# RWKV preparation of a two-block model: 24 parts on half-unit slots, and work moved between GpSimd, VectorE and ScalarE

## The chip, the cores and the metric

The kernel runs on one core of a Trainium2 chip. The metric is the device time of one execution in microseconds (us), the median of several runs. The core's engines run side by side, each with a queue of its own that it works off in order: PE (TensorE), DVE (VectorE), ACT (ScalarE), POOL (GpSimd) and SP, which here only starts DMAs.

## The reference

A model in fp32 with two blocks: block 1 (a pooling mixer and HGRN2) and block 2 (memory attention, a conformer convolution, a bidirectional RWKV-7 scan, an output projection, and a mixture of 16 experts chosen by the experts). The change lies in the RWKV scan of block 2, which for 6 heads of 64 and 1024 tokens computes, in both directions:

```python
def wkv7_scan(r, w, k, v, kk, a, reverse):
    def step(state, inp):
        r_t, w_t, k_t, v_t, kk_t, a_t = inp
        sa = jnp.einsum('bhij,bhj->bhi', state, -kk_t)
        state = (state * w_t[..., None, :]
                 + sa[..., :, None] * (kk_t * a_t)[..., None, :]
                 + v_t[..., :, None] * k_t[..., None, :])
        y_t = jnp.einsum('bhij,bhj->bhi', state, r_t)
        return state, y_t
...
    for d, (wd, ad) in enumerate(((wdf, adf), (wdb, adb))):
...
        k_d = heads(k * (1.0 + (a - 1.0) * k_a.astype(f32)))
        ys = wkv7_scan(r_tm, tm(heads(w)), tm(k_d), v_tm, kk_tm, tm(heads(a)), reverse=(d == 1))
        outs.append(jnp.moveaxis(ys, 0, 1))
        bonuses.append(jnp.sum(r_h * k_d * r_k32, axis=-1, keepdims=True) * v_h)
```

## The kernel before

The two directions run together, one on each half of the 128 partitions. The 1024 tokens are cut into 16 blocks of 64, which are the 16 **steps** of a chain: within a block the recurrence is solved with matrices, and only the state S (64x64 for each head) goes from one step to the next. Two steps make a **unit** g (0 to 7).

**`rwkv_prep`** (line 925) makes a unit's matrices ahead of its steps. It is a generator in 22 parts. Part 0 loads r, k, kk, a (L938) and the decay logs C (L940). Part 1 clears two blocks of AR on POOL (L943), sums C by a scan on DVE (L944), takes exponentials on ACT (L947, L948), forms kd on ACT (L950, six instructions) and multiplies it by k on POOL (L951). Parts 2 to 5 are products of 64 or 128 partitions by 768: AR (L955, L965, L966) and BK (L960, L969) on DVE; a times E (L956) and zz (L962, L963) on POOL. Parts 6 to 9 are the score matmuls on PE (L976), their copies Dt on ACT (L983) and the masked results on DVE (L984, L987). Part 10 writes Dt to DRAM (dD, L999, two DMAs), part 11 reads it back as the 96 triangular 16x16 blocks L (L1007), so that part 12 can invert them all at once: X is cleared on POOL (L1021, L1022), and 15 rounds of a product el (L1028) and a subtraction (L1030) follow. That elimination runs on the engine `el`: DVE for units 0 to 2, POOL for units 3 to 7 (`s.elp`). The inverses go out to DRAM (dX, L1033) and come back spread over 128 partitions (Xc, L1037, two DMAs). The rest builds the inverse M of each 64x64 block from them: Xs on ACT (L1040), a transpose (L1042), matmuls (L1051, L1057), a predicated copy (L1059), a transpose (L1061), four copies into M on DVE (L1063), two more matmuls (L1069, L1076) and the last copies into M on ACT (L1079).

**`rwkv_chain`** (line 1081) does the two steps of a unit: u = AR times A on PE (L1107), its copy us on ACT (L1110), sa = M times us (L1114), its copy B, one half on DVE (L1116) and one on ACT (L1117), then the new state's increment (L1121) and the output y (L1127), S on DVE (L1134, L1135), and the next step's A from S, half on DVE (L1136), half on ACT (L1137). So each step needs M of its unit at L1114, between us and B.

**The order.** `rwkv` (line 1146) walks over slots n, six to a unit, two yields of the chain in each; `s.lead[k]` says how many slots before the unit's first slot part k runs, and `s.fill` in which slots pieces of another stage, the output projection of attention and convolution (`mix_out_a`: loads, L869 and L149 to L151), come. The framework then reorders instructions within a window by its own priorities, so what stands in each engine's queue is shown below. Three register sets (`nset`) let units overlap. A unit's DMAs before the change all start on SP, in one queue with the loads of the next units, the loads of A and B (L1093) and the output writes.

After the last step the output normalisation of the last blocks, routing and the experts follow; they need all of the scan's output.

## Time and profile before

| | |
|---|---|
| median of 3 runs | 3227.86 us (3224.34 to 3228.44) |
| the profiled execution's own time | 3216.67 us |
| its span | 3214.9 us |
| busy over the span | PE 2997.3 (93%), DVE 2269.2 (71%), ACT 1254.0 (39%), POOL 264.8 (8%) |
| mean granted TensorE clock | 0.96 |
| first scan of unit 0 (L944) | 2121.8 us |
| state updates (L1134) | 15, the first at 2216.0, the last at 2480.7 us |

The profiled execution took 11.2 us less than the median. PE is at full speed nearly all the time outside the RWKV stretch; in it, from 2121.8 to about 2504 us, no engine is. A step lasts from 9 to 30 us, and the state update on DVE marks it.

### The profile page before, as it was taken

The numbers are of one execution on the slowest core, as the hardware profiler recorded it, in microseconds if no ns is written. First come the engines' busy times: TensorE is split into PE (matmuls) and PEld (weight loads), VectorE is DVE, ScalarE is ACT, GpSimd is POOL, SyncE is SP. The second block draws the span as 40 slices with busy tenths as digits, with TensorE's granted clock in tenths as the row PEclk, the third lists the DMA queues.
The fourth block names the chain that finished last, engine by engine and source line by source line (L and its number), as shares of the span: only waits on it lengthen the run. The fifth ranks groups of instructions, "written<-read, shape, count | busy, mean of one in ns | idle before, by whom it ended". The sixth has DMA issues, their size and how long they took to land.

```text
span 3214.9 us, 48713 instructions
## 1 busy us (share of the span) xinstructions
PE 2997.3 (93%) x20104; PEld 2457.3 (76%) x20104; DVE 2269.2 (71%) x2774; ACT 1254.0 (39%) x1598; POOL 264.8 (8%) x357
## 2 busy tenths in 40 slices
PE   8999999989999999999998899958878759999998
PEld 6888888778888888888887776646666548888776
DVE  5454545557686766867667897567676689999998
ACT  4221212233222222222223325533344348888777
POOL 0000000000000000000001100032362000000100
PEclk9999999999999999999999999979878779999999
DMA  4111111111111111111111524366744759999994
GB/s 131 46 53 46 47 46 59 40 34 34 40 34 53 41 34 40 34 51 36 40 40 53 130 69 148 115 194 195 196 117 129 280 219 383 383 389 390 379 364 161
DMA packets 349103, 423.88 MB, mean 132 GB/s; under 512 B 84816, under 2 KB 271824, under 8 KB 348880
## 3 DMA queue, kind: packets, MB, share of 16 engines
q1 hardware_dynamic: 342784, 399.26, 37.0%
q0 software_dynamic: 6096, 21.50, 2.5%
q8 instruction: 158, 2.59, 0.3%
q14 instruction: 65, 0.53, 0.1%
HBM read 359.96 MB, written 60.74 MB: 131 GB/s over the span
## 4 chain that ended last, share of the span: by engine, by line
PE 75%; DVE 10%; DMA 5%; ACT 3%; issue 3%; POOL 2%; SPq 1%; DVEq 0%; ACTq 0%; POOLq 0%
PE mm L159 14%; PE mm L161 14%; PE mm L157 14%; PE sc L157 4%; PE sc L161 4%; PE sc L159 4%; PE mm L149 3%; PE mm L151 3%; PE mm L150 3%; DVE cv L681 2%; DVE wl L102 2%; PE sc L404 1%; PE sc L481 1%; PE sc L471 1%; DMA wr<-in_w_e_down_dram 1%
## 5 line engine op out<-in xcount | busy, mean ns | idle before, releaser
L102 DVE TENSOR_TENSOR wl<-wr,wh 128x1024 fp32r<-128x1024 f32 x508 | 608.7, 1222 | 375.9 <-ACT wh L101 356.1
L101 ACT ACTIVATE wh<-wr 128x1024 fp32r<-128x1024 f32 x508 | 530.6, 1059 | 775.4 <-PE mm L159 549.7
L157 PE MATMUL mm<-hn,wh 128*128 128x512 f32 x1600 | 514.8, 395 | 3.3 <-ACT hn L195 1.7
L161 PE MATMUL mm<-hn,wl 128*128 128x512 f32 x1600 | 517.1, 395 | 0.0
L159 PE MATMUL mm<-hn,wh 128*128 128x512 f32 x1600 | 511.0, 394 | 0.0
L161 PEld LDWEIGHTS mm<-hn,wl 128*128 128x128 f32 x1600 | 300.3, 188 | 66.0 <-issue 5.3
L159 PEld LDWEIGHTS mm<-hn,wh 128*128 128x128 f32 x1600 | 300.1, 188 | 66.0 <-issue 4.8
L157 PEld LDWEIGHTS mm<-hn,wh 128*128 128x128 f32 x1600 | 299.7, 189 | 65.9 <-ACT hn L195 2.1
L240 DVE TENSOR_TENSOR h<-sc,h 128x1024 f32<-128x1024 f32 x192 | 229.8, 1219 | 90.2 <-PE sc L161 88.0
L159 PE MATMUL mm<-wl,th 128*128 128x512 f32 x768 | 245.8, 401 | 6.0 <-DVE wl L102 5.9
L157 PE MATMUL mm<-wh,th 128*128 128x512 f32 x768 | 240.3, 394 | 2.3 <-ACT th L101 2.3
L161 PE MATMUL mm<-wh,tl 128*128 128x512 f32 x768 | 238.3, 391 | 0.1
L159 PEld LDWEIGHTS mm<-wl,th 128*128 128x128 f32 x768 | 138.3, 188 | 47.1 <-DVE wl L102 20.8
L161 PEld LDWEIGHTS mm<-wh,tl 128*128 128x128 f32 x768 | 144.3, 188 | 32.2 <-DVE tl L102 0.5
L157 PEld LDWEIGHTS mm<-wh,th 128*128 128x128 f32 x768 | 142.8, 189 | 32.4 <-ACT th L101 2.9
L157 PE MATMUL sc<-oh,sh 128*128 128x512 f32 x512 | 163.2, 395 | 2.2 <-DVE h L240 2.2
L161 PE MATMUL sc<-oh,sl 128*128 128x512 f32 x512 | 159.1, 394 | 0.0
L159 PE MATMUL sc<-ol,sh 128*128 128x512 f32 x512 | 158.6, 391 | 0.0
L149 PE MATMUL mm<-wh,hn 128*128 128x256 f32 x512 | 147.0, 287 | 0.2 <-DVE gt L514 0.2
L151 PE MATMUL mm<-wh,hn 128*128 128x256 f32 x512 | 146.0, 285 | 0.0
L150 PE MATMUL mm<-wl,hn 128*128 128x256 f32 x512 | 145.4, 284 | 0.1
L101 ACT ACTIVATE oh<-wr 128x1024 fp32r<-128x1024 f32 x32 | 33.9, 1059 | 211.9 <-PE sc L161 199.5
(514 smaller groups left out, 4874.2 us busy)
## 6 DMA issues: line engine op xcount, KB each, us to landing
wr<-in_w_e_gate_dram SPq DMA_DIRECT2D x128, 512.0 KB, 7.8
wr<-in_w_e_up_dram SPq DMA_DIRECT2D x128, 512.0 KB, 6.6
wr<-in_w_e_down_dram SPq DMA_DIRECT2D x128, 512.0 KB, 6.4
wr<-in_hgrn_w_in_dram SPq DMA_DIRECT2D x64, 512.0 KB, 4.0
wr<-in_pool_w_in_dram SPq DMA_DIRECT2D x32, 512.0 KB, 4.0
wr<-in_w_in_dram SPq DMA_DIRECT2D x20, 512.0 KB, 3.8
wr<-in_pool_w_out_dram SPq DMA_DIRECT2D x16, 512.0 KB, 3.6
wr<-in_hgrn_w_out_dram SPq DMA_DIRECT2D x16, 512.0 KB, 3.6
```

Source lines behind the costliest of these rows:

```text
L101: s.act(hi, raw, AF.Copy)
L102: (eng or s.V).tensor_tensor(lo, raw, hi.bitcast(F32), op=OP.subtract)
L149: s.mm(o, ah, bh, start=first, stop=False)
L150: s.mm(o, ah, bl, start=False, stop=False)
L151: s.mm(o, al, bh, start=False, stop=last)
L157: s.mm(o, ah, bh[n], start=first, stop=False)
L159: s.mm(o, ah, bl[n], start=False, stop=False)
L161: s.mm(o, al, bh[n], start=False, stop=last)
L240: s.tt(h[i], o, h[i], op=OP.add)
L404: mm(o[r, c], lh[:, c * 128 + n * 64:c * 128 + n * 64 + 64], r3[:, 2 * c + n], start=True, stop=True)
L471: mm(pu[:, cs(c)], kt[:, cs(c)], v[:, c], start=True, stop=True)
L681: s.stt(acc, up[:, t:t + T], w, acc, op0=OP.mult, op1=OP.add)
```

## The change

It does five things.

1. The slots are halved: `lead` counts half slots (a part can now run at either yield of the chain), and the inverse is cut in three by two more yields (after rounds j = 4 and 9), which makes 24 parts. In half slots the numbers before were 30, 24, 24, 24, 24, 22, 22, 20, 16, 14, 14, 14, 6, 6, 6 and seven times 2. `fill` is doubled, which leaves its places.
2. The products kd, a times E and zz go from POOL to DVE (zz behind the masks).
3. `s.elp` is empty: the elimination of every unit runs on DVE.
4. The four copies into M and DVE's half of B go to ACT.
5. The inverse's DMAs (dD, L, dX, Xc, six for each unit) start from POOL's queue rather than SP's.

POOL keeps the memsets. Line numbers move by one up to the scan and by three or so behind it.

```diff
@@ -41,14 +41,15 @@
         s.cnat, s.dmc, s.dmv, s.dmt = 5, s.P.dma_start, s.dma, s.P.dma_start
         s.ahead, s.npf = [], 1
         s.ready = {3: 33, 4: 30, 2: 37, 5: 37, 1: 43, 6: 42}
-        s.elp = (3, 4, 5, 6, 7)
+        s.elp = ()
         s.wo_at, s.wo_done = 38, False
         s.ylast, s.fast, s.dmy = {}, 42, s.dma
         s.nraw, s.nraw2 = 17, 11
         s.n = 0
+        s.dmi = s.P.dma_start
         s.spr, s.nset = 6, 3
-        s.lead = (15, 12, 12, 12, 12, 11, 11, 10, 8, 7, 7, 7, 3, 3, 3, 1, 1, 1, 1, 1, 1, 1)
-        s.fill = (-10, -10, -8, -8, -7, -4, -3, -2, 1, 2, 2, 2, 3, 4, 4, 7, 8, 8, 9, 9, 10)
+        s.lead = (30, 24, 24, 23, 22, 22, 21, 20, 19, 18, 17, 15, 13, 12, 11, 10, 8, 6, 5, 4, 3, 2, 1, 1)
+        s.fill = (-20, -20, -16, -16, -14, -8, -6, -4, 2, 4, 4, 4, 6, 8, 8, 14, 16, 16, 18, 18, 20)
         s.ct = (5, 5, 8)
         s.nye, s.nhid, s.nwh = 1, 2, 3
         s.nsum = 4
@@ -948,19 +949,16 @@
         act(E, C[:, :, 1:], AF.Exp, scale=0.606531)
         for h in range(6):
             act(kd[:, h], a[:, h], AF.Identity, scale=s.rka[:, h:h + 1], bias=s.rkam[:, h:h + 1])
-        s.P.tensor_tensor(kd, x["k"], kd, op=OP.mult)
+        tt(kd, x["k"], kd, op=OP.mult)
         yield
         s.V.tensor_copy(sc.rearrange("p c h -> p h c"), P.rearrange("p (h c) t -> p h c t", c=2)[:, :, :, 64])
         for d, r in enumerate(s.halves):
             tt(AR[r, :, d, 0], u3(x["kk"])[r], P[r, :, 0:64], op=OP.mult)
-        s.P.tensor_tensor(u3(a), u3(a), E, op=OP.mult)
+        tt(u3(a), u3(a), E, op=OP.mult)
         yield
         BK = s.tl(p, "BK", 2, (128, 12, 2, 64))
         for d, r in enumerate(s.halves):
             tt(BK[r, :, 1 - d], u3(kd)[r], E[r], op=OP.mult)
-        zz = s.tl(p, "zz", 1, (128, 6, 128))
-        s.P.tensor_tensor(zz[0:64], x["r"][0:64], kd[0:64], op=OP.mult)
-        s.P.tensor_tensor(rev(zz[64:128]), x["r"][64:128], kd[64:128], op=OP.mult)
         yield
         tt(AR[0:64, :, 0, 1], u3(x["r"])[0:64], P[0:64, :, 1:], op=OP.mult)
         tt(rev(AR[64:128, :, 1, 1]), u3(x["r"])[64:128], P[64:128, :, 1:], op=OP.mult)
@@ -993,10 +991,13 @@
             nx = scores(q + 1) if q < 2 else None
             masked(q, o)
             o = nx
+        zz = s.tl(p, "zz", 1, (128, 6, 128))
+        tt(zz[0:64], x["r"][0:64], kd[0:64], op=OP.mult)
+        tt(rev(zz[64:128]), x["r"][64:128], kd[64:128], op=OP.mult)
         yield
         dD = s.tl(s.dp, "dD", 2, (2, 12 * 4160))
         for d, r in enumerate(s.halves):
-            s.dma(bass.AP(tensor=dD.tensor, offset=dD.offset + d * 12 * 4160, ap=[[64, 64], [4160, 12], [1, 64]]), Dt[r])
+            s.dmi(bass.AP(tensor=dD.tensor, offset=dD.offset + d * 12 * 4160, ap=[[64, 64], [4160, 12], [1, 64]]), Dt[r])
         os = []
         for q in range(2):
             os.append(g_((128, 4, 128)))
@@ -1004,7 +1005,7 @@
                 s.PE.transpose(os[q][:, c], BK[:, 4 * q + c].rearrange("p n t -> p (n t)"), s.ident)
         yield
         L = s.tl(p, "L", 1, (96, 16, 16))
-        s.dma(L, bass.AP(tensor=dD.tensor, offset=dD.offset, ap=[[1040, 96], [64, 16], [1, 16]]))
+        s.dmi(L, bass.AP(tensor=dD.tensor, offset=dD.offset, ap=[[1040, 96], [64, 16], [1, 16]]))
         for q in range(2):
             act(TK[:, 4 * q:4 * q + 4], os[q], AF.Copy)
         o, o1 = g_((128, 4, 128)), g_((128, 6, 2))
@@ -1028,13 +1029,15 @@
             el.tensor_tensor(zv, L[:, j:j + 1, j + 1:].to_broadcast([96, n, m]),
                              X[:, 0:n, j:j + 1].to_broadcast([96, n, m]), op=OP.mult)
             el.tensor_tensor(X[:, 0:n, j + 1:], X[:, 0:n, j + 1:], zv, op=OP.subtract)
+            if j in (4, 9):
+                yield
         yield
         dX = s.tl(s.dp, "dX", 2, (96, 256))
-        s.dma(dX, X.rearrange("p a b -> p (a b)"))
+        s.dmi(dX, X.rearrange("p a b -> p (a b)"))
         yield
         Xc, Xs = s.tl(p, "Xc", 1, (128, 12, 16)), s.tl(p, "Xs", 1, (128, 12, 32))
         for d, r in enumerate(s.halves):
-            s.dma(Xc[r], bass.AP(tensor=dX.tensor, offset=dX.offset + d * 48 * 256, ap=[[16, 64], [1024, 12], [1, 16]]))
+            s.dmi(Xc[r], bass.AP(tensor=dX.tensor, offset=dX.offset + d * 48 * 256, ap=[[16, 64], [1024, 12], [1, 16]]))
         yield
         for n in range(2):
             act(Xs[:, :, n * 16:n * 16 + 16], Xc, AF.Copy, scale=s.m16[:, n:n + 1])
@@ -1060,7 +1063,7 @@
         Xt = s.tl(p, "Xt", 1, (128, 12, 32))
         s.V.transpose(f2(Xt), f2(Xf))
         for n, r in enumerate(quads):
-            s.V.tensor_copy(M[r, :, n % 2 * 32:n % 2 * 32 + 32], Xf[r])
+            act(M[r, :, n % 2 * 32:n % 2 * 32 + 32], Xf[r], AF.Copy)
         yield
         ys = s.tl(p, "ys", 1, (128, 12, 32))
         o = i_()
@@ -1113,7 +1116,7 @@
             for h, d, r in heads:
                 mm(sa[r, h], M[r, 2 * h + c], uv[r, h], start=True, stop=True)
             yield
-            s.V.tensor_copy(B[0:64, 0], sa[0:64])
+            act(B[0:64, 0], sa[0:64], AF.Copy)
             act(B[64:128, 1], sa[64:128], AF.Copy)
             yield
             so = s.tl(ps, "c", 1, (128, 6, 64))
@@ -1146,11 +1149,11 @@
     def rwkv(s, ps, psc, rb, ry):
 
 
-        lead = s.lead
+
         at = {}
         for g in range(8):
-            for k, l in enumerate(lead):
-                at.setdefault(s.spr * g - l, []).append((k, g))
+            for k, l in enumerate(s.lead):
+                at.setdefault(2 * s.spr * g - l, []).append((k, g))
         preps = [s.rwkv_prep(g, ps) for g in range(8)]
         with s.pool("RF", "right") as pf:
             out = s.mix_out_a(psc, pf)
@@ -1164,12 +1167,13 @@
             for n in range(min([*at, *s.fill]), 0):
                 parts(n)
             chain = (x for g in range(8) for x in s.rwkv_chain(g, psc))
-            last = max(s.fill) + 1
+            last = max(s.fill) // 2 + 1
             n = 0
             while n < last:
                 next(chain)
-                parts(n)
+                parts(2 * n)
                 next(chain)
+                parts(2 * n + 1)
                 n += 1
             for _ in out:
                 pass
@@ -1181,7 +1185,7 @@
                 live.remove(b)
 
         for _ in chain:
-            parts(n)
+            parts(2 * n)
             if n == s.wo_at:
                 live.insert(0, s.mix_weights())
             live += [s.mix_block(i, ps, psc) for i, at_ in s.ready.items() if at_ == n]
@@ -1196,6 +1200,7 @@
                 s.prefetch(s.npf)
             step()
             next(chain)
+            parts(2 * n + 1)
             if n >= s.fast:
                 step()
             n += 1
```

In each excerpt a name is a buffer (its number tells instances apart), and the bracket is what the instruction waits for.

**POOL**, before: the end of unit 4's elimination, then the memsets and products of the next unit, and the elimination of unit 5.

```order
L1028 TENSOR_TENSOR el_17512<-L_17301,X_17470 96x28 [waits Pool_49]
L1030 TENSOR_TENSOR X_17470<-X_17470,el_17512 96x14x2 [waits Pool_49]
L1028 TENSOR_TENSOR el_17515<-L_17301,X_17470 96x15 [waits Pool_49]
L1030 TENSOR_TENSOR X_17470<-X_17470,el_17515 96x15 [waits Pool_49]
L1021 MEMSET X_18471 96x256 [waits DMAHW5_49,Pool_49]
L1022 MEMSET X_18471 96x16 [waits Pool_49]
L943 MEMSET AR_1662_14919 64x12x64 [waits PE_49,Pool_49]
L943 MEMSET AR_1662_14919 64x12x64 [waits PE_49]
L951 TENSOR_TENSOR kd_17833<-xk_17526,kd_17833 128x768 [waits DVE_49,DMAHW2_49,Activation_49,Pool_49]
L956 TENSOR_TENSOR xa_17530<-xa_17530,EX_17832 128x768 [waits DMAHW4_49,DVE_49]
L962 TENSOR_TENSOR zz_17850<-xr_17524,kd_17833 64x768 [waits DMAHW1_49,PE_49,Pool_49]
L963 TENSOR_TENSOR zz_17850<-xr_17524,kd_17833 64x6x128 [waits Pool_49]
```

And now, around the same units: DMAs and memsets only.

```order
L1008 DMA L_17202<-dD_17117 96x16x16 [waits DMASW7_49,DMASW6_49,DMASW2_49]
L1000 DMA dD_17607<-Dt_17434 64x12x64 [waits Activation_49] x2
L944 MEMSET AR_1662_14919 64x12x64 [waits PE_49] x2
L1008 DMA L_17692<-dD_17607 96x16x16 [waits DMASW1_49,DMASW2_49,DMASW0_49,DVE_49]
L1036 DMA dX_17428<-X_17330 96x256 [waits DMASW4_49,DVE_49]
L1040 DMA Xc_17486<-dX_17428 64x12x16 [waits DMASW5_49,DMASW4_49]
L1040 DMA Xc_17486<-dX_17428 64x12x16
```

The eliminations and products have left the queue; a unit's DMAs stand behind the next unit's memsets and behind the wait of its read L.

**DVE**, before: around the copy B of one step of the chain and the state update behind it.

```order
L869 TENSOR_TENSOR ax_16352<-ax_16352,a_16354 128x512 [waits DMAHW3_49,DMAHW2_49,PE_49]
L1116 COPY B_16317<-c_16518 64x384 [waits PE_49]
L869 TENSOR_TENSOR ax_16376<-ax_16376,a_16468 128x512 [waits DMAHW5_49,DMAHW1_49,PE_49]
L1042 STREAM_TRANSPOSE Xt_16627<-Xs_16455 128x384 [waits Activation_49]
L984 TENSOR_TENSOR RBK_1663_14920<-g_16531,mkI_13002 128x512 [waits PE_49,Activation_49]
L987 TENSOR_TENSOR AR_1662_14919<-g_16531,mkS_13001 64x4x64 x2
L1134 TENSOR_TENSOR S_16827<-c_16581,S_16378 128x384 [waits PE_49]
L1135 TENSOR_TENSOR S_16827<-S_16827,rsc_1671_14931 128x384 [waits DVE_49]
L1136 COPY A_16619<-S_16827 64x384 [waits DVE_49]
```

And now, in the elimination of unit 4, around the state update of step 6 (S_17500):

```order
L1029 TENSOR_TENSOR el_17367<-L_17202,X_17330 96x64 [waits DVE_49]
L1137 TENSOR_TENSOR S_17500<-c_17442,S_17288 128x384 [waits PE_49]
L1031 TENSOR_TENSOR X_17330<-X_17330,el_17367 96x8x8 [waits DVE_49]
L1138 TENSOR_TENSOR S_17500<-S_17500,rsc_1666_14923 128x384 [waits DVE_49]
L1029 TENSOR_TENSOR el_17370<-L_17202,X_17330 96x63 [waits DVE_49]
L1139 COPY A_17480<-S_17500 64x384 [waits DVE_49]
L1031 TENSOR_TENSOR X_17330<-X_17330,el_17370 96x9x7 [waits DVE_49]
L952 TENSOR_TENSOR kd_17871<-xk_17547,kd_17871 128x768 [waits Activation_49]
L1029 TENSOR_TENSOR el_17373<-L_17202,X_17330 96x60 [waits DVE_49]
L982 TENSOR_TENSOR RBK_1673_14936<-g_17490,mkI_13002 128x512 [waits PE_49,Activation_49]
```

The copy of B is gone from DVE, and the rounds of an elimination alternate with the state update, products and masks.

**ACT**, before: the copy us of step 7, and Xs of the unit that step 8 needs, ahead of step 7's B (B_17431).

```order
L1110 ACTIVATE us_17534<-c_17452 128x384 [waits PE_49,Activation_49]
L947 ACTIVATE PX_17831<-C_17532 128x780 [waits DMAHW6_49,DVE_49]
L948 ACTIVATE EX_17832<-C_17532 128x768
L1040 ACTIVATE Xs_17521<-Xc_17520,m_1405_13014 128x12x16 [waits DMAHW2_49,DMAHW1_49]
L1117 ACTIVATE B_17431<-c_17536 64x384 [waits DVE_49]
L1040 ACTIVATE Xs_17521<-Xc_17520,m_1405_13014 128x12x16
```

And now: the end of step 7 (its A), the copy us of step 8, and then the Xs that step 8 needs.

```order
L1140 ACTIVATE A_17746<-S_17778 64x384 [waits DVE_49]
L1113 ACTIVATE us_17885<-c_17838 128x384 [waits PE_49,Activation_49]
L1043 ACTIVATE Xs_17487<-Xc_17486,m_1405_13014 128x12x16 [waits DMASW6_49,DMASW5_49]
L1043 ACTIVATE Xs_17487<-Xc_17486,m_1405_13014 128x12x16
L1046 ACTIVATE Xf_17534<-Xs_17487 128x384 [waits Activation_49]
L948 ACTIVATE PX_18359<-C_18043 128x780 [waits DMAHW3_49,DVE_49]
L949 ACTIVATE EX_18360<-C_18043 128x768
```

Xs of that unit (4) stands one step of the chain later than before; units 6 and 7 have theirs directly behind A of steps 11 and 13, where before it stood ahead of that step's B.

## Rows read from the trace of the kernel before

**Rows 1.** Windows: us; PE, PEld, DVE, ACT, POOL busy; PE clock; DMA share; GB/s

```profile
2121.80:2216.00 94.20, 67.22 (x601) 51.87 (x603) 79.70 (x139) 30.57 (x68) 34.75 (x26) 0.80 0.66 185
2305.00:2386.00 81.00, 56.22 (x1150) 46.39 (x1146) 54.23 (x76) 35.02 (x80) 47.49 (x90) 0.73 0.49 127
2386.00:2480.70 94.70, 77.85 (x1726) 62.05 (x1721) 68.30 (x137) 42.42 (x96) 32.08 (x68) 0.86 0.47 129
sum 358.90, PE 282.28 PEld 224.19 DVE 261.37 ACT 140.71 POOL 140.44; mean PE 70.57 PEld 56.05 DVE 65.34 ACT 35.18 POOL 35.11
```

**Rows 2.** Chain of waits, 2305 to 2386: share by engine and line

```profile
by line: issue 30.4%; POOL X L1030 10.7%; POOL el L1028 9.8%; PE g L976 7.5%; DMA xk<-dk 6.5%; DMA C<-dw 4.6%; POOL xa L956 3.1%; POOL kd L951 2.4%; DVE A L1136 2.3%; POOL zz L962 2.3%; PE c L1114 2.3%; POOL zz L963 2.3%; DVE rsc L953 2.1%;
```

**Rows 3.** Groups by line on POOL, 2100 to 2504: us busy, mean ns | idle before

```profile
L1030 POOL TENSOR_TENSOR X<-X,el 96x15 f32<-96x15 f32 (+7 forms) x75 | 29.4, 392 | 5.9
L1028 POOL TENSOR_TENSOR el<-L,X 96x15 f32<-96x15 f32 (+7 forms) x75 | 26.1, 348 | 25.7 <-DMA L<-dD 19.9
L951 POOL TENSOR_TENSOR kd<-xk,kd 128x768 f32<-128x768 f32 x8 | 17.9, 2237 | 79.0 <-ACT kd L950 62.1 <-issue 16.8
```

**Rows 4.** The same groups on DVE

```profile
L960 DVE TENSOR_TENSOR BK<-kd,EX 64x768 f32<-64x768 f32 x16 | 21.0, 1312 | 1.1 <-POOL kd L951 0.8
L969 DVE TENSOR_TENSOR BK<-xkk,xa 64x768 f32<-64x768 f32 x16 | 19.4, 1210 | 0.2
L955 DVE TENSOR_TENSOR AR<-xkk,PX 64x768 f32<-64x768 f32 x16 | 18.7, 1171 | 0.2
L1063 DVE COPY M<-Xf 32x384 f32<-32x384 f32 x32 | 16.1, 504 | 0.4
L1030 DVE TENSOR_TENSOR X<-X,el 96x15 f32<-96x15 f32 (+7 forms) x45 | 13.1, 292 | 1.3
L965 DVE TENSOR_TENSOR AR<-xr,PX 64x768 f32<-64x768 f32 x8 | 10.6, 1326 | 0.1
L1028 DVE TENSOR_TENSOR el<-L,X 96x15 f32<-96x15 f32 (+7 forms) x45 | 10.5, 232 | 3.4 <-DMA L<-dD 2.3
L966 DVE TENSOR_TENSOR AR<-xr,PX 64x768 f32<-64x768 f32 x8 | 9.2, 1147 | 0.2
L1116 DVE COPY B<-c 64x384 f32<-64x384 f32 x16 | 8.8, 548 | 19.5 <-PE c L1114 19.3
```

**Rows 5.** Lines of DVE: min/median/max ns; a product, and unit 1's inverse

```profile
L955 DVE TENSOR_TENSOR AR<-xkk,PX x16: 940/955/2474, 2125.1 to 2395.1; 64x768 f32<-64x768 f32 x16
L1028 DVE TENSOR_TENSOR el<-L,X x15: 170/204/220, 2194.7 to 2201.7; 96x15 f32<-96x15 f32 x2, 96x28 f32<-96x28 f32 x2, 96x39 f32<-96x39 f32 x2, 96x48 f32<-96x48 f32 x2
L1030 DVE TENSOR_TENSOR X<-X,el x15: 170/205/221, 2194.9 to 2202.0; 96x15 f32<-96x15 f32 x2, 96x28 f32<-96x28 f32 x2, 96x39 f32<-96x39 f32 x2, 96x48 f32<-96x48 f32 x2
```

**Rows 6.** Waits of DVE and of SP's queue, 2216 to 2481: us, times, longest

```profile
DVE B L1116 <- PE c L1114: 17.4, 9, 5.4
DVE C L944 <- DMA C<-dw: 9.2, 4, 5.2
SPq L1033 <- POOL X L1030: 36.0, 5, 12.9
```

**Rows 7.** A group by line on ACT, 2100 to 2504

```profile
L1117 ACT ACTIVATE B<-c 64x384 f32<-64x384 f32 x16 | 7.8, 486 | 28.1 <-DVE B L1116 28.0
```

**Rows 8.** DMA issues: queue, KB each, median us to landing

```profile
dX<-X SPq DMA_DIRECT2D x8, 96.0 KB, 2.1
Xc<-dX SPq DMA_DIRECT2D x16, 48.0 KB, 2.9
dSh<-ath POOLq DMA_DIRECT2D x8, 128.0 KB, 2.2
```

**Rows 9.** Issue time of that POOL DMA, ns, min/median/max

```profile
L841 POOL DMA_DIRECT2D dSh<-ath x8: 718/723/937, 1920.9 to 2095.3; - x8
```

**Rows 10.** Unit 6's Xs and the state updates of steps 11 and 12

```profile
L1040 ACT ACTIVATE Xs<-Xc,m x2: 438/446/454, 2423.2 to 2423.6; 128x192 f32<-128x192 f32 x2
L1134 DVE TENSOR_TENSOR S<-c,S x2: 558/558/558, 2431.9 to 2449.1; 128x384 f32<-128x384 f32 x2
```

## The prediction

> **What bounds the kernel now.** I read the windows of the RWKV stretch first, since everything that the change touches lies between the first scan (2121.8 us) and the last state update (2480.7 us); what follows waits for all of the scan's output, and so only shifts. In these 358.9 us no engine is full: PE is busy 282.28, DVE 261.37, ACT and POOL 140 each [rows 1]. DVE thus stands idle for 97.5 us. Its share is not even: 79.70 of 94.20 us (85%) before the first state update, 54.23 of 81.00 (67%) from 2305 to 2386, 68.30 of 94.70 (72%) after that. In the middle stretch POOL has its peak, 47.49 us.
>
> Next I read the chain of waits there. POOL's own steps make up 30.6% of the 81 us: X 10.7, el 9.8, xa 3.1, kd 2.4, and the two halves of zz 2.3 each, so 24.8 us [rows 2]. The loads xk and C stand on it with 11.1%, 9.0 us; why a load is late is told by the waits of SP's queue: the write dX waits five times for POOL's last X, 36.0 us in all, up to 12.9 at once [rows 6], and the next unit's loads stand behind it in that queue. "Issue" (30.4%) is time for which the profile shows no releaser; I give it to nobody.
>
> Third, the groups by line. On POOL a round of the elimination takes 392 + 348 = 740 ns and a product 2237 [rows 3]; on DVE, in unit 1, a round takes 205 + 204 = 409 ns, and a product 955 in the median [rows 5]. But DVE's products are slower in the mean than in the median, 1147 to 1326 ns, and their longest is 2474 [rows 4, 5]: they are stretched while POOL runs its own.
>
> **The change part by part.** The sum is made for DVE, the engine that takes over the work, as busy time that comes and goes and as waits that go.
>
> *Comes.* The products: four for each of eight units, at the median of 955 ns, 32 x 0.955 = +30.6 us. That a POOL product covers 128 partitions and the DVE row 64 makes no difference to the length along a partition, 768. The elimination of units 3 to 7: 75 rounds x 0.409 = +30.7.
>
> *Goes.* The copies of M, -16.1, and DVE's half of B, -8.8 [rows 4]. The stretching, since POOL keeps only memsets: mean less 955, times the count, is 5.7 for L960, 4.1 for L969, 3.5 for L955, 3.0 for L965, 1.5 for L966; and DVE's own elimination of units 0 to 2, 10.5 + 13.1 us for 45 rounds against 45 x 0.409 = 18.4, gives 5.2. Together -23.0. So DVE's busy time grows by 61.3 - 24.9 - 23.0 = **+13.4 us**.
>
> *Waits that go.* From 2216 us on DVE stood 17.4 us in B for the matmul of sa, the largest wait that it has, and 9.2 us in the scan for the load of C [rows 6]. The first leaves DVE with the copy; the second is late through SP's queue, which loses dX. Together **-26.6 us**. If they are not simply gone, the next to be late behind B is the state update, which waits for the chain as well; behind the loads, the exponentials on ACT.
>
> *ACT.* Its half of B waited 28.0 us for DVE's half [rows 7]: the two halves of one tile already run one behind the other. On ACT they take 486 + 486 instead of 548 + 486, so the chain gains 0.06 x 16 = 1 us, or loses what ACT's queue holds ahead of them; I take 0. The four M copies take 4 x 0.486 = 1.9 us there against 4 x 0.504 = 2.0 on DVE: 0 too. What hides the 32 x 0.486 + 16 x 0.486 = 23 us that ACT takes over is that it is busy 140.71 of 358.9; were it full at that place, all of a unit's 1.9 us would be on the chain, 16 us at worst.
>
> *The DMAs on POOL.* A direct DMA of POOL's in the stage before takes 723 ns to issue and 2.2 us to land, for 128 KB [rows 8, 9]; the nearest of SP is dX, 2.1 for 96 KB. So I take 0.1 us more of landing and 0.2 more for each of the three issues of dX and Xc in a unit (an estimate; SP's issues were shorter than 0.7), 0.7 us in all, in the five units whose elimination was late on POOL: **+3.5 us**. Upwards: POOL's row is for 256 pieces of 512 bytes, an Xc has 768 of 64; if issuing grows with the pieces, an Xc takes 3 x 0.723 = 2.2 us, which is 1.45 more for each of two, so 3.6 us for a unit and 18 for five. Downwards: they no longer stand in SP's queue between the loads, which I count at nothing beyond the wait of C.
>
> A rule speaks against this part. The rows show POOL's DMA issuing in 718 to 937 ns and nothing that held it up [rows 9]. The Trainium skill (SBUF — State Buffer, SBUF: two separate sides, the trap "DVE blocks DMA") says that POOL cannot write the descriptors of its DMAs while VectorE runs a copy from SBUF to SBUF in fp32, and advises to start such DMAs from SP or ACT. By it, each of three DMAs of a unit could wait for one more copy of 0.5 us, 12 us over the eight units, and the sum would be about +2; by the row, it is what stands next. No run yet shows these DMAs beside DVE's copies.
>
> *The half slots.* They cost nothing themselves; what they do is in the order. The eliminations now stand among state updates, masks and products, so that one lasts longer from end to end than its 15 x 0.409 = 6.1 us of work. I price that at 0 because DVE does due work in between, and let it decide a rival.
>
> *Sum.* 13.4 - 26.6 + 3.5 = **-9.7 us**. The profiled execution took 3216.67 us, which would be 3207.0; its own time lies 11.2 us under the median, so against the median of 3227.86 I forecast **3218 us**.
>
> **The rivals.**
>
> *More than that comes off (faster, about 3199).* If POOL's steps truly set the pace from 2305 us on, DVE's speed (409 for 740 ns, 955 for 2237) takes 45 to 57% of the 24.8 us, some 12, off that stretch; 12 x 32.08 / 47.49 = 8 off the next one, by POOL's busy time in both [rows 1]; and the 9.0 us of loads leave the chain: -29, which is 3199. For it: POOL's share of the chain [rows 2]. Against it: what else DVE must do in that time.
>
> *Nothing comes of it (no change, about 3227).* The wait for sa is a wait for the chain; if half of its 17.4 us comes back in the state update, the sum is -9.7 + 8.7 = -1.0, so 3227. For it: the chain's links are on PE and ACT, and the change makes none of them shorter. Against it: the state update's line is not among the large waits now.
>
> *M comes a step later (slower, about 3235).* The place is Xs on ACT, from which M follows. In unit 6 Xs started at 2423.2, ahead of the state update of step 11 (2431.9), and step 12's update, which needs M, came at 2449.1, 25.9 us after Xs, while steps 11 to 12 took 17.2 [rows 10]. In the order now, Xs of units 4, 6 and 7 stands behind the A copy of the odd step. If Xs to state update remains 25.9 us, the even step takes that long instead of 17.2 in units 6 and 7 (unit 4's step 8 is already as long): 2 x 8.7 = 17.4, which makes -9.7 + 17.4 = +7.7, so 3235.6. It is slower by over 0.2% from 8.1 us for each of the two units on. For it: the order says so. Against it: the 25.9 us held a step of the chain in between, so that the bare way is shorter, and the step after it finds DVE free. This is also the case in which the change does not do what it says, because the parts that are spread over half slots end later and not earlier.
>
> *POOL's DMAs are dear (slower, about 3239).* With the upper price, 18 us instead of 3.5, and the read L late as well by about one Xc (2 us in three units, 6), the sum is -9.7 + 14.5 + 6 = +10.8 and the time 3239. It is slower by over 0.2% once the DMAs cost 20 us. For it: six DMAs of a unit in one queue, each with its waits, behind memsets that wait for PE. Against it: the row of POOL's DMA. By the skill's rule alone, with its 12 us, it would be 3230, no change.
>
> **How the numbers follow.** A measurement of this kernel can tell about 0.2%, 6.5 us, from no change. My forecast of -9.7 has a chance of 0.31 and the larger gain 0.15: faster 0.46. No change has 0.22. M a step later has 0.22 and dear DMAs 0.10: slower 0.32. The range reaches from 3187, the larger gain with 12 more where the rest of the wait for C and of POOL's share goes, to 3248, where M's delay (+7.7) and the dear DMAs (+14.5) come to 3250 together; outside I leave 2 in 10. For the cases of faster alone it would be 3190 to 3221.
>
> **What would show it.** Right: no product on DVE over 1.1 us; DVE busy about 275 us between the first scan and the last state update, and that stretch shorter by 10; no wait of the loads for dX. Wrong: even steps (to the state updates of steps 12 and 14) over 24 us; Xc landing later than 4 us after its issue; DVE waiting in the state update for more than 10 us in all. If the first stretch, to the first state update, grows by over 5 us, DVE was full there and the products cost more than I took.

## The result, and the profile after

The changed kernel took 3192.76 us (median of 4 runs, 3188.16 to 3200.31) against 3226.1 for the one before, measured beside it; the ratio is 0.9899, with a 95% interval from 0.9884 to 0.9914. That is 33 us less, 28 to 37 by the interval. The forecast was 3218, 10 us less, in a range that holds the result; the direction was right and the size was three times too small. The profiled execution of the changed kernel took 3188.16 us with a span of 3186.4, against 3216.67 and 3214.9.

| stretch, us | before | after |
|---|---|---|
| start to the first scan of unit 0 | 2121.8 | 2125.0 |
| to the first state update | 94.2 | 98.1 |
| to the fifth | 89.1 | 78.3 |
| to the ninth | 80.9 | 68.3 |
| to the last, the fifteenth | 94.7 | 87.2 |
| from there to the end | 734.2 | 729.5 |

From the first scan to the last state update 27.0 us came off, all of them behind the first update; with 4.7 behind the last and 3.2 lost ahead of the scan that makes the 28.5 us between the two executions. A second profiled execution of the changed kernel, which took 3196.34 us, has 339.7 us in place of 331.9 for the whole stretch, so a single profile tells its length to some 8 us. The windows of these four stretches, as [rows 1] (us; PE, PEld, DVE, ACT, POOL busy; granted clock; DMA share; GB/s):

```profile
2125.00:2223.10 98.10, 70.38 (x619) 53.58 (x620) 79.50 (x156) 39.56 (x87) 10.02 (x16) 0.84 0.83 235
2223.10:2301.40 78.30, 71.07 (x1296) 58.60 (x1293) 55.09 (x128) 36.16 (x83) 12.95 (x20) 0.98 0.72 196
2301.40:2369.70 68.30, 53.78 (x1130) 44.73 (x1130) 56.56 (x138) 38.74 (x88) 12.90 (x20) 0.81 0.51 139
2369.70:2456.90 87.20, 74.58 (x1730) 58.72 (x1728) 65.57 (x179) 52.12 (x113) 10.55 (x14) 0.91 0.46 134
sum 331.90, PE 269.82 PEld 215.63 DVE 256.72 ACT 166.57 POOL 46.43; mean PE 67.45 PEld 53.91 DVE 64.18 ACT 41.64 POOL 11.61
```

DVE is busy 256.72 us where it had 261.37 [rows 1], although it took over POOL's eliminations and products; its idle time fell from 97.5 to 331.9 - 256.7 = 75.2. POOL went from 140 to 46 us. PE is busy 269.82 instead of 282.28 us for the same matmuls, at a higher granted clock in each stretch. The groups on DVE, as [rows 4]:

```profile
L1029 DVE TENSOR_TENSOR el<-L,X 96x15 f32<-96x15 f32 (+7 forms) x120 | 23.6, 197 | 13.0 <-DMA L<-dD 10.9
L1031 DVE TENSOR_TENSOR X<-X,el 96x15 f32<-96x15 f32 (+7 forms) x120 | 23.5, 196 | 2.1
L967 DVE TENSOR_TENSOR BK<-xkk,xa 64x768 f32<-64x768 f32 x16 | 15.2, 950 | 0.3
L961 DVE TENSOR_TENSOR BK<-kd,EX 64x768 f32<-64x768 f32 x16 | 15.2, 948 | 0.2
L956 DVE TENSOR_TENSOR AR<-xkk,PX 64x768 f32<-64x768 f32 x16 | 15.1, 946 | 0.2
L952 DVE TENSOR_TENSOR kd<-xk,kd 128x768 f32<-128x768 f32 x8 | 7.6, 946 | 3.8 <-ACT kd L951 3.8
```

No product is stretched any more: every line of them takes 937 to 956 ns in the mean and none of them more than 959, and a round of the elimination 197 + 196 ns. The waits of DVE and of SP's queue, as [rows 6]:

```profile
DVE Xt L1045 <- ACT Xs L1043: 9.3, 5, 6.7
DVE S L1137 <- PE c L1124: 5.8, 5, 2.7
SPq L1096 <- PE y L1130: 50.3, 8, 22.4
```

The wait for sa (17.4 us) is gone from DVE's list, and of the wait for the load of C (9.2) 0.2 us is left. SP's queue holds no dX any more, and so no 36.0 us of waiting for an elimination's last X; its long wait now stands ahead of the loads of A and B (L1096), for PE's matmuls of y. The inverse's DMAs, as [rows 8]:

```profile
dD<-Dt POOLq DMA_DIRECT2D x16, 192.0 KB, 4.4
L<-dD POOLq DMA_DIRECT2D x8, 96.0 KB, 6.0
dX<-X POOLq DMA_DIRECT2D x8, 96.0 KB, 3.5
Xc<-dX POOLq DMA_DIRECT2D x16, 48.0 KB, 3.4
```

They land later than they did on SP's queue, in the median dX in 3.5 us instead of 2.1, Xc in 3.4 instead of 2.9.

### The profile page after: what moved, and what is told of

Read it like the earlier page. It is cut to its first block, busy times and chain, and to the rows that moved or that the text cites. A ratio compares the mean times of both kernels' runs of the same rounds, so it can differ in the third digit from the quotient of the medians.

```text
span 3186.4 us, 48716 instructions
## 1 busy us (share of the span) xinstructions
PE 2982.2 (94%) x20104; PEld 2445.8 (77%) x20104; DVE 2262.5 (71%) x2908; ACT 1279.5 (40%) x1646; POOL 176.5 (6%) x223
## 4 chain that ended last, share of the span: by engine, by line
PE 76%; DVE 10%; issue 5%; DMA 5%; ACT 3%; SPq 1%; POOL 1%; ACTq 0%; POOLq 0%; DVEq 0%
PE mm L160 14%; PE mm L162 14%; PE mm L158 14%; PE sc L158 4%; PE sc L162 4%; PE sc L160 4%; PE mm L150 3%; PE mm L152 3%; PE mm L151 3%; DVE cv L682 2%; PE sc L405 1%; DVE wl L103 1%; PE sc L482 1%; PE sc L472 1%; PE sc L1433 1%
## 5 line engine op out<-in xcount | busy, mean ns | idle before, releaser
L102 ACT ACTIVATE wh<-wr 128x1024 fp32r<-128x1024 f32 x508 | 530.5, 1059 | 776.0 <-PE mm L160 563.0
L102 ACT ACTIVATE oh<-wr 128x1024 fp32r<-128x1024 f32 x32 | 33.9, 1059 | 212.8 <-PE sc L162 200.6
```

The costliest lines, as they stand in the source:

```text
L102: s.act(hi, raw, AF.Copy)
```

## The experiments

All ratios are to the kernel before, measured beside each kernel, with their 95% intervals. The changed kernel itself was run twice: 0.9899 (0.9884 to 0.9914), and once more beside the second group below:

> The changed kernel once more, to have its time beside the runs of this call: both theories 0.9899 of the one before, 0.987 to 0.993.

It gave 0.9891 (0.9865 to 0.9917), 3191.47 us.

**One part undone.** Each of the first four takes one part of the change back and leaves the rest.

The elimination of units 3 to 7 back on GpSimd:

```diff
-        s.elp = ()
+        s.elp = (3, 4, 5, 6, 7)
```

> The changed kernel (33 us under the one before) with the elimination of units 3 to 7 back on GpSimd. Theory POOL (GpSimd's steps set the pace, and its instructions stretch VectorE's products): half of the gain is lost, about 3210 us. Rival QUEUE (the gain comes from the loads and the inverse's DMAs no longer standing in one queue, and from the order): the elimination is off the path, the time stays within 8 us of 3193. Rival DVE (VectorE is the bound, and gets 31 us of work back): faster than the changed kernel, 3185 or less.

0.9964 (0.9951 to 0.9978), 3211.76 us: two thirds of the gain lost, where theory POOL had said half; both rivals fall. Its rows of the elimination on POOL:

```profile
L1031 POOL TENSOR_TENSOR X<-X,el 96x15 f32<-96x15 f32 (+7 forms) x75 | 34.6, 462 | 5.9
L1029 POOL TENSOR_TENSOR el<-L,X 96x15 f32<-96x15 f32 (+7 forms) x75 | 29.6, 395 | 22.5 <-DMA L<-dD 17.0
```

A round takes 857 ns, where it took 740 [rows 3], beside a DVE that now runs all products. DVE's products stay at 940 to 959 ns in the mean there and none takes over 984, although 22 of the 96 ran at the same time as an instruction of POOL's elimination. So it is POOL's own products, and not the elimination, that stretched them in the kernel before.

The products back on GpSimd:

```diff
-        tt(kd, x["k"], kd, op=OP.mult)
+        s.P.tensor_tensor(kd, x["k"], kd, op=OP.mult)
...
-        tt(u3(a), u3(a), E, op=OP.mult)
+        s.P.tensor_tensor(u3(a), u3(a), E, op=OP.mult)
...
-        tt(zz[0:64], x["r"][0:64], kd[0:64], op=OP.mult)
-        tt(rev(zz[64:128]), x["r"][64:128], kd[64:128], op=OP.mult)
+        s.P.tensor_tensor(zz[0:64], x["r"][0:64], kd[0:64], op=OP.mult)
+        s.P.tensor_tensor(rev(zz[64:128]), x["r"][64:128], kd[64:128], op=OP.mult)
```

> The changed kernel with the products kd, a times E and zz back on GpSimd. Theory POOL: VectorE's products are stretched again (mean 1.15 to 1.3 us instead of 0.95, some 18 us) and kd comes later; 10 to 18 us of the gain are lost, 3203 to 3211. Rival QUEUE: the products are hidden, within 8 us of 3193. Rival DVE (it gets 30 us of work back): 3185 or less.

0.9965 (0.9953 to 0.9978), 3210.77 us: again some 20 us lost, a little more than theory POOL said; the rivals fall. On DVE the stretching is back, in the products and in the chain's own state update:

```profile
L961 DVE TENSOR_TENSOR BK<-kd,EX 64x768 f32<-64x768 f32 x16 | 19.9, 1246 | 8.9 <-POOL kd L952 8.7
L1138 DVE TENSOR_TENSOR S<-S,rsc 128x384 f32<-128x384 f32 x15 | 10.2, 679 | 0.1
```

The inverse's DMAs back on SP's queue:

```diff
-        s.dmi = s.P.dma_start
+        s.dmi = s.dma
```

> The changed kernel with the inverse's six DMAs of a unit back on SP's queue. Theory QUEUE: the loads stand behind the writes that wait for the elimination again, 10 us or more of the gain are lost, 3203 or more. Theory POOL: SP no longer waits for a slow GpSimd, so it is within 8 us of 3193. Rival DEAR DMAs (on GpSimd's queue they land 0.5 to 2 us later each, on the path to M): 3185 or less.

0.9912 (0.9891 to 0.9933), 3196.08 us. The interval overlaps that of the changed kernel: no loss that can be measured. The loss of 10 us that theory QUEUE set as its least would be 0.9930, at the very edge of the interval, so little is left of QUEUE; DEAR DMAs, which said faster, falls. Two further kernels split this:

```diff
-            s.dmi(bass.AP(tensor=dD.tensor, offset=dD.offset + d * 12 * 4160, ap=[[64, 64], [4160, 12], [1, 64]]), Dt[r])
+            s.dma(bass.AP(tensor=dD.tensor, offset=dD.offset + d * 12 * 4160, ap=[[64, 64], [4160, 12], [1, 64]]), Dt[r])
...
-        s.dmi(L, bass.AP(tensor=dD.tensor, offset=dD.offset, ap=[[1040, 96], [64, 16], [1, 16]]))
+        s.dma(L, bass.AP(tensor=dD.tensor, offset=dD.offset, ap=[[1040, 96], [64, 16], [1, 16]]))
```

> The changed kernel with dD and L (three DMAs of a unit, ahead of the elimination) on SP's queue, dX and Xc left on GpSimd's. On GpSimd's queue L landed in 6.0 us, on SP's in 2.9. If the read L is late (VectorE waited 10.9 us for it), it gains up to 8 us: 0.987 to 0.990; if the loads wait behind dD in SP's queue, it loses up to 8: 0.990 to 0.993.

```diff
-        s.dmi(dX, X.rearrange("p a b -> p (a b)"))
+        s.dma(dX, X.rearrange("p a b -> p (a b)"))
...
-            s.dmi(Xc[r], bass.AP(tensor=dX.tensor, offset=dX.offset + d * 48 * 256, ap=[[16, 64], [1024, 12], [1, 16]]))
+            s.dma(Xc[r], bass.AP(tensor=dX.tensor, offset=dX.offset + d * 48 * 256, ap=[[16, 64], [1024, 12], [1, 16]]))
```

> The changed kernel with dX and Xc on SP's queue, dD and L left on GpSimd's. On GpSimd's queue dX landed in 3.5 and Xc in 3.4 us, on SP's in 1.7 and 2.8: 2.4 us for each unit on the way to M. If that sets the even steps of units 4, 6 and 7, it gains 5 to 10 us: 0.986 to 0.9885; if SP's wait for the end of the elimination holds up the loads behind it, it loses 3 to 10: 0.991 to 0.994.

They gave 0.9912 (0.9892 to 0.9932) and 0.9915 (0.9893 to 0.9938). Neither is a version to prefer, and neither can be told from the changed kernel: that these DMAs land earlier from SP's queue brings nothing that can be measured.

The copies of M and of B back on VectorE:

```diff
-            act(M[r, :, n % 2 * 32:n % 2 * 32 + 32], Xf[r], AF.Copy)
+            s.V.tensor_copy(M[r, :, n % 2 * 32:n % 2 * 32 + 32], Xf[r])
...
-            act(B[0:64, 0], sa[0:64], AF.Copy)
+            s.V.tensor_copy(B[0:64, 0], sa[0:64])
```

> The changed kernel with the four copies of M and VectorE's half of B back on VectorE. By the sum on VectorE (25 us of work and the wait of B, 17 us, come back, of which ScalarE loses 24): 8 to 15 us of the gain are lost, 3201 to 3208. Rival (VectorE has room, and both halves of B ran one behind the other anyway): within 6 us of 3193.

0.9972 (0.9960 to 0.9984), 3215.41 us: the largest loss of all in the median, though its interval overlaps those of the two before, and over the upper end of what was expected. The copy of B alone:

```diff
-            act(B[0:64, 0], sa[0:64], AF.Copy)
+            s.V.tensor_copy(B[0:64, 0], sa[0:64])
```

> The changed kernel with only VectorE's half of B back on VectorE. Both copies back cost 17 to 24 us. If the chain's wait in VectorE's queue is what costs (theory B), this alone loses 12 us or more: ratio 0.9935 or more. If it is the M copies in VectorE's queue (theory M), it stays within 6 us: 0.990 to 0.992.

0.9921 (0.9896 to 0.9946): 3198.79 us, some 7 more than the changed kernel measured beside it, between the two theories and inside both intervals. So by the medians the larger part of the loss comes with the M copies. With both back, DVE waits 25.4 us for the chain's matmuls between its first and its last state update, where the changed kernel has 5.8:

```profile
DVE B L1119 <- PE c L1117: 13.6, 8, 5.6
DVE S L1137 <- PE c L1124: 11.8, 7, 2.5
```

That the copies stand in turn behind eliminations and products in DVE's queue, on the way to M, is how I read the rest; it was not tried apart.

The places of the parts as before:

```diff
-        s.lead = (30, 24, 24, 23, 22, 22, 21, 20, 19, 18, 17, 15, 13, 12, 11, 10, 8, 6, 5, 4, 3, 2, 1, 1)
+        s.lead = (30, 24, 24, 24, 24, 22, 22, 20, 16, 14, 14, 14, 6, 6, 6, 6, 6, 2, 2, 2, 2, 2, 2, 2)
```

> The changed kernel with the places of the parts as before (all numbers of the lead doubled, the inverse's three parts together). If the half slots only follow the engines (theory ENGINES), it stays within 8 us of the changed kernel: ratio up to 0.9925. If VectorE can take the elimination only where it is started earlier and spread (theory SLOTS), 15 us or more are lost: 0.9945 or more.

0.9946 (0.9927 to 0.9966), 3205.92 us: 14 us more than the changed kernel measured beside it, at the limit that theory SLOTS set and outside that of ENGINES.

**One part alone.** Three kernels go the other way. First only the half slots and 24 parts, with engines, copies and DMAs as before:

```diff
-        s.elp = ()
+        s.elp = (3, 4, 5, 6, 7)
...
-        s.dmi = s.P.dma_start
+        s.dmi = s.dma
...
-        tt(kd, x["k"], kd, op=OP.mult)
+        s.P.tensor_tensor(kd, x["k"], kd, op=OP.mult)
...
-            act(M[r, :, n % 2 * 32:n % 2 * 32 + 32], Xf[r], AF.Copy)
+            s.V.tensor_copy(M[r, :, n % 2 * 32:n % 2 * 32 + 32], Xf[r])
...
```

> Only the half slots and the 24 parts (and zz behind the masks): elimination and products on GpSimd, copies on VectorE, DMAs on SP as before. Theory ENGINES: within 8 us of the one before, 0.9975 to 1.0025. Theory SLOTS: half of the gain or more without any move between engines, 0.995 or less.

1.0027 (1.0016 to 1.0038), 3234.07 us: 9 us slower than before, just beyond what theory ENGINES allowed, so the slots by themselves gain nothing. The chain of waits from the fifth state update to the last, in the kernel before (2305 to 2481 us) and in this one (2317 to 2503), and this one's wait of SP's queue for dX:

```profile
by line: issue 17.6%; POOL X L1030 11.8%; POOL el L1028 10.7%; PE g L976 5.2%; PE y L1127 4.3%; PE c L1114 3.8%; DMA xk<-dk 3.0%; DMA Xc<-dX 2.9%; PE c L1121 2.5%; POOL zz L963 2.4%; DMA dX<-X 2.4%; PE i L1051 2.3%; POOL zz L962 2.1%; DMA C
```

```profile
by line: issue 16.8%; POOL el L1029 15.4%; POOL X L1031 15.1%; DMA Xc<-dX 3.8%; PE c L1117 2.5%; POOL xa L957 2.4%; POOL zz L996 2.3%; DMA dX<-X 2.2%; PE c L1110 2.2%; PE y L1130 2.2%; DMA h<-in_w_out_dram 2.1%; POOL zz L995 2.0%; DMA dD<-D
```

```profile
SPq L1036 <- POOL X L1031: 53.6, 5, 17.6
```

POOL's elimination is 30.5% of the chain here, where it was 22.5%, and dX holds up SP for 53.6 us, where it was 36.0 [rows 6]: with the elimination on POOL, spreading the parts did not help.

Next, in the kernel before, only the elimination and the products moved to VectorE:

```diff
-        s.elp = (3, 4, 5, 6, 7)
+        s.elp = ()
...
-        s.P.tensor_tensor(kd, x["k"], kd, op=OP.mult)
+        tt(kd, x["k"], kd, op=OP.mult)
...
-        s.P.tensor_tensor(u3(a), u3(a), E, op=OP.mult)
+        tt(u3(a), u3(a), E, op=OP.mult)
...
-        s.P.tensor_tensor(zz[0:64], x["r"][0:64], kd[0:64], op=OP.mult)
-        s.P.tensor_tensor(rev(zz[64:128]), x["r"][64:128], kd[64:128], op=OP.mult)
+        tt(zz[0:64], x["r"][0:64], kd[0:64], op=OP.mult)
+        tt(rev(zz[64:128]), x["r"][64:128], kd[64:128], op=OP.mult)
```

> The kernel before with only the elimination of units 3 to 7 and the products kd, a times E and zz moved to VectorE; places of the parts, copies and DMAs as before. If the parts of the change add up (each worth its own), 15 us or more are gained here: ratio 0.995 or less. If VectorE can only take this with the copies off it and the parts spread (theory TOGETHER), it is no faster than before: 0.998 or more.

0.9914 (0.9880 to 0.9947), 3197.76 us. **This part alone gives a gain that can't be told from that of the whole change**, with the old slots, the copies on DVE and the DMAs on SP. Its interval is wide, 17 to 39 us of gain. Theory TOGETHER falls. Its windows, from the first state update on, with the sum over all four stretches:

```profile
2214.70:2291.30 76.60, 74.48 (x1290) 59.53 (x1287) 58.25 (x125) 29.37 (x67) 3.38 (x6) 0.98 0.77 212
2291.30:2361.90 70.60, 55.47 (x1163) 44.39 (x1161) 63.43 (x156) 37.11 (x84) 3.90 (x8) 0.81 0.57 150
2361.90:2457.50 95.60, 77.86 (x1713) 62.19 (x1711) 74.67 (x210) 42.85 (x93) 1.90 (x4) 0.83 0.54 156
sum 333.70, PE 275.59 PEld 218.43 DVE 274.57 ACT 145.05 POOL 10.63; mean PE 68.90 PEld 54.61 DVE 68.64 ACT 36.26 POOL 2.66
```

DVE is busy 274.57 us, more than in either kernel, and its idle time is 59 us instead of 97.5: the work fitted into the gaps. The M copies, left on DVE, shortened by themselves:

```profile
L1063 DVE COPY M<-Xf 32x384 f32<-32x384 f32 x32 | 10.9, 340 | 0.4
```

And only the copies, in the kernel before:

```diff
-            s.V.tensor_copy(M[r, :, n % 2 * 32:n % 2 * 32 + 32], Xf[r])
+            act(M[r, :, n % 2 * 32:n % 2 * 32 + 32], Xf[r], AF.Copy)
...
-            s.V.tensor_copy(B[0:64, 0], sa[0:64])
+            act(B[0:64, 0], sa[0:64], AF.Copy)
```

> The kernel before with only the four copies of M and VectorE's half of B moved to ScalarE. If they are worth by themselves what undoing them cost (17 to 24 us), the ratio is 0.9945 or less; theory TOGETHER: VectorE has idle time in the kernel before (97 of 359 us), so at most 8 us: 0.9975 or more.

0.9992 (0.9979 to 1.0005): no difference, as TOGETHER said of this part. Its sum over the same four stretches:

```profile
sum 357.60, PE 281.04 PEld 222.65 DVE 243.46 ACT 162.68 POOL 138.54; mean PE 70.26 PEld 55.66 DVE 60.86 ACT 40.67 POOL 34.64
```

DVE lost 17.9 us of work against the kernel before and stood idle for nearly as much longer, 114.1 us instead of 97.5.

What follows: undone one at a time, the parts cost 0.65%, 0.66%, 0.13%, 0.73% and 0.47% of the time (ratio less 0.9899), 2.6% together, where the whole change is worth 1.0%. Done one at a time they are worth 0.86% (POOL emptied), 0.08% (copies, with an interval from -0.05 to 0.21%) and -0.27% (slots). Only the first gains alone. The copies and the places cost what undoing them costs only inside the new order; undo slots, copies and DMAs all at once, and the loss is again within the intervals. Why the parts depend on each other in this way was not shown. No kernel had a lower median than the changed one.

## Why the prediction was right, and where its size was not

**What bounds the kernel.** Right: POOL's steps stood on the path, and DVE's idle time could take them in. The run that empties POOL and does nothing else shows it.

**What the sum is made of.** The step that failed is the one before its terms: "the sum is made for DVE", as busy time and waits. The runs show that DVE's busy time is not what sets the time. With POOL alone emptied DVE is busy 18 us longer than in the changed kernel, and the stretch is 333.7 us against 331.9. With the elimination back on POOL it is busy 21 us less, and the stretch is 25.4 us longer:

```profile
sum 357.30, PE 279.71 PEld 227.61 DVE 235.85 ACT 164.55 POOL 111.64; mean PE 69.93 PEld 56.90 DVE 58.96 ACT 41.14 POOL 27.91
```

The two terms that brought the sum under zero are worth nothing by themselves. The kernel with only the copies moved loses both the copies and the wait for sa on DVE; by the sum that is -24.9 - 17.4 = -42 us, and measured it was no difference. The part that does gain, the elimination and the products, stands in the sum as +61.3 - 23.0 = +38.3 us, less at most 9.2 for the load of C; alone it took 28 us off. What it took off was POOL's steps, 24.8 us of the chain in one stretch, which the prediction had read and left out of its sum. So the direction was right by the reading of the chain and, in the sum, by luck.

**Comes.** 30.6 us for the products, measured 32 x 0.947 = 30.3. The elimination on DVE grew from 23.6 us [rows 4] to 47.1, +23.5, where the sum had 25.5. Both right as work for DVE.

**Goes.** The copies, -24.9, as said. The stretching of the product lines was right too: it is 18.1 us, where the sum had 17.8. But the sum stopped at those lines and the elimination, and other lines of DVE lost theirs as well: the state update's second half, DVE's copy A and the copy rsc, before and after:

```profile
L1135 DVE TENSOR_TENSOR S<-S,rsc 128x384 f32<-128x384 f32 x15 | 9.9, 663 | 0.3
L1136 DVE COPY A<-S 64x384 f32<-64x384 f32 x15 | 6.9, 459 | 0.3
L953 DVE COPY rsc<-PX 128x12 f32<-128x12 f32 x8 | 3.2, 394 | 3.0 <-ACT PX L947 3.0
```

```profile
L1138 DVE TENSOR_TENSOR S<-S,rsc 128x384 f32<-128x384 f32 x15 | 8.2, 545 | 0.1
L1139 DVE COPY A<-S 64x384 f32<-64x384 f32 x15 | 5.2, 348 | 0.1
L954 DVE COPY rsc<-PX 128x12 f32<-128x12 f32 x8 | 1.3, 165 | 0.0
```

These three took 5.3 us less, and the product al (L102, 809 to 679 ns) 1.3. DVE's busy time in the stretch fell by 4.7 us, where the sum had +13.4, 18 us off. Some 10 of them are no work at all: records of DVE's instructions overlap where one does not need the result of the one before, and busy time counts the overlap once. Here X ends at 2389.87 us, after y has begun:

```profile
2389.65 0.22 DVE L1031 TENSOR_TENSOR X<-X,el 96x63 f32<-96x63 f32 x1
2389.79 0.55 DVE L1285 TENSOR_TENSOR y<-y,y 128x384 f32<-128x384 f32 x1
```

Added up by their durations, DVE's instructions over the whole span take 2381.1 us before and 2384.6 after, +3.5, while the busy time falls from 2269.2 to 2262.5. Against +3.5 the sum is 10 us too high: 6.6 for the four lines, 2.0 for the elimination and the rest in small amounts.

**Waits that go.** 26.6 us was forecast. The wait for sa and nearly all of the wait for C went, and from the first state update on DVE's idle time fell from 83.0 to 56.6 us, by 26.4. That this agrees is luck: the wait for sa goes just as well in the kernel with only the copies moved, and there the idle time grew. The half of B's wait that the no-change rival brought back came to 5.8 us in the state update, where it had been 2.7, below the 10 us at which I would have called it wrong.

**A term that was not in the sum: TensorE's clock.** From the first state update to the fifth PE is nearly full, and the stretch is as long as its matmuls take. Before:

```profile
2216.00:2305.10 89.10, 81.10 (x1297) 63.98 (x1294) 59.24 (x108) 32.70 (x75) 26.20 (x32) 0.90 0.75 211
```

After, the same matmuls took 71.07 us at a granted clock of 0.98, and the stretch 78.3. That is 10.8 of the 27 us. All four stretches show more clock after (0.84, 0.98, 0.81, 0.91 against 0.80, 0.90, 0.73, 0.86), and so do the first three of the kernel with POOL alone emptied (0.83, 0.98, 0.81; the fourth has 0.83). These 10 us windows of PE in the kernel before show one fall of the clock (us, busy, clock, DMA share, GB/s). It was at 1.00, the upper level of 2.4 GHz, while PE was busy for 9.95 us; in the next window PE was busy for 4.72 us, and in the one after that the clock stood at 0.50, the lower level of 1.2 GHz.

```profile
2306.00:2316.00 10.00, 9.95 (x132) 1.00 0.49 124
2316.00:2326.00 10.00, 4.72 (x243) 0.69 0.90 239
2326.00:2336.00 10.00, 5.65 (x136) 0.50 0.44 108
2336.00:2346.00 10.00, 5.68 (x77) 0.61 0.28 80
2346.00:2356.00 10.00, 6.27 (x74) 1.00 0.50 125
```

PE stood idle for 76.6 of 358.9 us before [rows 1] and for 62.1 of 331.9 after. What the clock goes with can be seen in the changed kernel itself. In its second profiled execution the last of the four stretches has the granted clock 0.85 instead of 0.91; the same matmuls took 79.34 instead of 74.58 us there, and the stretch 91.4 instead of 87.2.

```profile
2371.10:2462.50 91.40, 79.34 (x1729) 62.88 (x1728) 65.75 (x178) 52.19 (x113) 10.56 (x14) 0.85 0.45 130
```

No run set the clock by itself, so how much of the 10.8 us is clock and how much is order stays open.

**The DMAs on POOL.** The term was +3.5 us, 0.7 for each of five units, of which 0.1 was landing. Landing measured +1.4 for dX, +0.5 for Xc and +2.1 for L; the issue of an Xc is 754 ns, near the low end, so issuing did not grow threefold with the pieces. By these rows the term was some three times too small, and yet undoing it gained nothing.

The rule of the Trainium skill (SBUF — State Buffer, SBUF: two separate sides, "DVE blocks DMA") needs a copy of VectorE's from SBUF to SBUF in fp32 beside the DMA. In the changed kernel the M copies are gone from VectorE, and none of the 48 issues of these DMAs met one of the copies that are left, so it could not show. Below are the issue times of Xc there, and then, with the copies of M and B back on VectorE, those of Xc and of the copies A and M:

```profile
L1040 POOL DMA_DIRECT2D Xc<-dX x16: 748/754/776, 2199.1 to 2437.7; - x16
```

```profile
L1040 POOL DMA_DIRECT2D Xc<-dX x16: 748/761/963, 2193.9 to 2461.7; - x16
L1139 DVE COPY A<-S x15: 310/351/558, 2228.8 to 2485.7; 64x384 f32<-64x384 f32 x15
L1066 DVE COPY M<-Xf x32: 304/351/674, 2210.8 to 2475.8; 32x384 f32<-32x384 f32 x32
```

The one issue of 963 ns, at 2427.2 us, stood beside a copy A of the usual 347 ns: there the trace agrees with that rule of the Trainium skill, at a cost of 0.2 us. In four other meetings it was the copy that took longer: two of M at 2211 us took 674 and 662 ns beside issues of Xc that took 748 to 767, and two of A, at 2357 and 2389 us, took 558 and 532. In the rest neither did, and copies B, which read PSUM, always took 541 to 551 ns. The 12 us that the prediction priced by the rule could not come in the changed kernel, and with the copies back the issues of Xc lost 0.2 us in all.

**The signs I named.** Of the signs for right, no product took over 1.1 us, and no load waited for dX; but DVE's busy time was not about 275 us but 256.7, and the stretch was shorter by 27 and not by 10. Of the signs for wrong, the step to the state update of step 12 took over 24 us, and five of the sixteen Xc, all in the first three units, landed later than 4 us, the latest after 6.8. The first stretch grew by 3.9 and not by over 5.

**M a step later.** This rival's mechanism came, as the order had it: Xs of unit 6 now stands behind step 11's state update, and the step after it is long.

```profile
L1043 ACT ACTIVATE Xs<-Xc,m x2: 439/439/439, 2408.7 to 2409.0; 128x192 f32<-128x192 f32 x2
L1137 DVE TENSOR_TENSOR S<-c,S x2: 558/558/558, 2403.8 to 2430.4; 128x384 f32<-128x384 f32 x2
L1137 DVE TENSOR_TENSOR S<-c,S x2: 557/557/557, 2437.5 to 2456.8; 128x384 f32<-128x384 f32 x2
```

Steps 11 to 12 took 26.6 us instead of 17.2, and 13 to 14 19.3 instead of 16.7. The rival's price was 8.7 for each of two; it was 9.4 and 2.6. What it left out is the steps around them: 9 to 10 took 11.2 us instead of 19.9, 10 to 11 10.5 instead of 16.0, 12 to 13 7.1 instead of 15.0. The whole stretch is 7.5 us shorter, so the delay was there and more was gained around it. The delay does not need the half slots, to which the rival gave it. The kernel with POOL alone emptied has the old places, and there Xs of unit 6 (2412.7 us) also stands behind step 11's state update (2401.5), and steps 11 to 12 take 27.7 us. With the half slots and the elimination on POOL, Xs (2424.2) stands ahead of it (2435.5), and the step takes 10.3.

**The larger gain.** The rival at 3199, with half of POOL's share of the chain and the 9.0 us of loads, came nearest in size, and its mechanism is the one that the runs bear out: POOL's steps set the pace. That moving both the elimination and the products gains is shown; how much of it is DVE's speed, how much the stretching that ends and how much the loads is not. With the elimination on DVE, the queue of the inverse's DMAs made no measurable difference.

## What to carry to other kernels

Do not add up the busy time of an engine that has idle time and take the sum for the kernel's time. Here VectorE took over 54 us of work and the time fell, and 25 us of copies taken off it alone changed nothing. What counted was which engine's steps stood in the chain of waits. When two engines stretch each other's instructions, as here, price a move by all the lines of the engine that stays, not only by those of the same kind. To know what a part of a tuned bundle is worth, do it alone as well as undo it alone: undone, the copies cost 0.73% and the places 0.47%; done alone, the copies gained nothing that could be measured, and the places lost. And where TensorE nearly fills a stretch, look at its granted clock before and after: it can move with a change that was made for another engine.

## What was not expected of the hardware

The stretching works both ways, but not for every pair. Beside GpSimd's products VectorE's took up to 2.58 us instead of 0.95 in the kernel before (L960). Beside GpSimd's small instructions of the elimination they kept their length, and it was GpSimd's round that went from 740 to 857 ns. And GpSimd's queue issued DMAs of 768 pieces of 64 bytes in 754 ns, hardly more than the 723 ns of 256 pieces [rows 9], while L with 1536 pieces took 996; their landing, 3.4 to 6.0 us, grew more than the issue.
